# Second halves of two-engine operations are put off to the next background step, in a two-part transformer kernel on one core

## The chip, the cores and the metric

The kernel runs on one core of one Trainium2 chip, in one launch. The metric is device microseconds from start to end of the launch, lower is better. TensorE is called PE in the profile, VectorE DVE, ScalarE ACT, GpSimd POOL and SyncE SP.

## The reference

One sequence of 512 tokens of width 1024 goes through two stacks, all in fp32. The first has two layers, each with a feed-forward block, a hybrid mixer (causal attention with forget gates beside a depthwise convolution), a second feed-forward block and a gated per-layer embedding. The second has four branches, one each: a state-space layer (s5), sliding-window attention (swa), causal attention with latent queries and keys (mla) and a spatial gating unit (sgu). Cut to its frame:

```python
def first_block(x, p, ...):
    h = x
    for i in range(2):
        h = h + 0.5 * swiglu(rmsnorm(h, g_ff1[i]), w_ff1_in[i], w_ff1_out[i])
        h = h + hybrid_mixer(rmsnorm(h, g_mix[i]), w_in[i], ...)
        h = h + 0.5 * swiglu(rmsnorm(h, g_ff2[i]), w_ff2_in[i], w_ff2_out[i])
        h = h + sigmoid(rmsnorm(h, g_ple[i]) @ w_ple_gate[i]) * (p[i] @ w_ple_proj[i])
    return rmsnorm(h, g_final)

def second_block(x, ...):
    for i, branch in enumerate((s5, swa, mla, sgu)):
        x = x + rmsnorm(branch(rmsnorm(x, pre_norm[i])), post_norm[i])
    return x
```

swiglu has 2816 hidden channels, so its second product sums over 22 blocks of 128.

## The kernel before, in words

Activations lie transposed, as 8 tiles of 128 channels by 512 tokens (`h`), and every dense product is made of 128x128 weight blocks against 512 tokens. To keep fp32 accuracy each operand is split into a high part and a low part, and each block product is three matmuls (`mm3`): L449 high weight by high data, L450 high weight by low data, L451 low weight by high data.

**Weights** are streamed in units of 8 blocks. `_dma` loads a unit into `raw` (three buffers). `_split` makes the two parts: ACT copies it into `whi` (L406), then DVE subtracts to get `wlo` (L407 in the code; in the profile all DVE operations go through one wrapper and show as L248). The two parts have three buffers each. `block` hands out the next block; when a unit is used up, `_advance` goes to the next unit and first calls `_ahead`, which splits up to two units beyond the one that starts.

**Epilogues** follow the tiles: after the matmuls of one output tile, `after_tile` runs small chains of DVE and ACT operations on its result. Many of them end in `split` (ACT makes the high part, DVE the low part), so that the next product can use the result. In the second product of a feed-forward block the epilogue adds the tile to `h` on DVE and then prepares the next block's operand (`prep`): high part on ACT (L715), low part on DVE, square on ACT, sum on DVE.

**Background steps.** Generators (attention, convolution, the scan of s5) are advanced by `step` after each tile and by `fine`, which `mtile` calls after the blocks 1, 3 and 5 of a tile, but only of a tile of 6 or 8 blocks. The 22-block tiles of the second feed-forward product call neither inside a tile. Neither does the head of `tiles`: there, after the branches s5, swa and mla, the first three tiles of the next branch are computed for the first 256 tokens, one after the other, and between them `one`, `two` and `rest` issue the norm of the branch before for the other 256 tokens; then the three tiles are computed for those (L514 to L527).

**Order.** The program is scheduled by hand: each engine executes its instructions in the order in which the Python code issues them. An instruction whose operand isn't ready holds up all that stand behind it on its engine. So the place at which the code issues an instruction is the place it has in its queue.

Of the kernel before, what the change touches and what calls it, by code (L numbers as in the profile page):

```python
# [291 lines left out]
class Kern:  # L292
# [3 lines left out]
    def __init__(self, ctx, tc, t, outT):  # L296
        self.tc, self.nc, self.t, self.outT = tc, tc.nc, t, outT
        nc = self.nc
        self.v = Vector(self, nc.vector)
        self.pe_n = self.dve_n = 0.0  # L300
        self.force = False
        pool = lambda n, b, **k: ctx.enter_context(tc.tile_pool(name=n, bufs=b, **k))
        self.cp = pool("const", 1)
        self.rawp = pool("raw", 3)
        self.wp = pool("wsplit", 3)
        self.sp = pool("slots", 1)
        self.smp = pool("small", 4)
# [18 lines left out]
        self.tables, self.M8, self.tabbed = {}, {}, []  # L326


# [64 lines left out]
    def _split(self):  # L393
        i = self.spli
        r = self.raws.pop(i)
        if self.units[i][1]:
            hl = self.slots(2), self.slots(2)
            self.kept.append(hl)
        else:
            hl = [[self.wp.tile([P, UB * P], F32, tag=n, name=self.nm(n))] for n in ("whi", "wlo")]  # L400
        self.sps[i] = self.r(hl)
        self.spli += 1
        w = UB * P // len(hl[0])

        def piece(hi, lo, src):
            self.nc.scalar.copy(hi.bitcast(F32R), src)  # L406
            self.v.tensor_tensor(lo.bitcast(F32R), src, hi, op=ALU.subtract)  # L407
        if i == 0:
            a, b = slice(0, w // 2), slice(w // 2, w)
            piece(hl[0][0][:, a], hl[1][0][:, a], r[:, a])  # L410
            return lambda: piece(hl[0][0][:, b], hl[1][0][:, b], r[:, b])
        for j, (hi, lo) in enumerate(zip(*hl)):
            piece(hi, lo, r[:, j * w:(j + 1) * w])
# [12 lines left out]
    def _advance(self, hold=0):  # L426
        self._ahead(self.ui, hold)
        self.cur = self.sps.pop(self.ui)
        self.ui += 1
        self.blkpos = 0  # L430
# [118 lines left out]
    def step(self):  # L549
# [5 lines left out]
        self.fine()  # L555

    def fine(self):
        for g in list(self.fines):
            if next(g, self) is self:
                self.fines.remove(g)  # L560
# [17 lines left out]
    def run_hooks(self):  # L578
        while self.hooks:
            self.hooks.popleft()()  # L580
        self.flush()
        while self.lazy:
            self.lazy.popleft()()


    def split(self, src, hi, lo, scale=None):
# [4 lines left out]
        else:  # L591
            nc.scalar.activation(hi.bitcast(F32R), src, AF.Copy, scale=scale)  # L592
            self.v.scalar_tensor_tensor(out=lo.bitcast(F32R), in0=src, scalar=scale, in1=hi,
                                           op0=ALU.mult, op1=ALU.subtract)

    @staticmethod
    def r(hl):
# [3 lines left out]

    def silu(self, ps, times=1.0):
# [3 lines left out]
        self.v.scalar_tensor_tensor(out=y, in0=t, scalar=1.0, in1=y, op0=ALU.add, op1=ALU.mult)  # L606
        self.free(t)
        return y

# [237 lines left out]
    def mixer(self, l, nxt):  # L847
# [61 lines left out]
        for p in range(4):  # L909
            for dst, sc in ((Q, -0.125), (K, None)):  # L910
                ps = self.mtile(Xr)

                def epi(ps=ps, dst=dst, sc=sc):
                    t, hi, lo = self.slot(), self.slot(), self.slot()
                    v.tensor_tensor(t, ps, self.rbc, op=ALU.mult)
                    self.split(t, hi, lo, sc)
                    self.free(t)
                    dst.append((hi, lo))
                self.after_tile(epi)
# [69 lines left out]
    def causal(self, n, ready, can_pv, begin, score, values, lags):  # L989
        nc, v = self.nc, self.v  # L990
        C = (self.slot(), self.slot())
        for t in C:
            nc.gpsimd.memset(t[:, 0:P], 0.0)
        todo, box, own = {}, {}, {}

# [3 lines left out]
        def scores(h, i):  # L999
# [5 lines left out]
            pr = own[h][0][:, P:] if i == 2 else own[h][-1]  # L1005
            mn, sm = (self.small([P, 1], tag=n, bufs=8) for n in ("mn", "sm"))
            score(h, i, pr, mn)
            box[h][0].append(pr)
            box[h][1].append((mn, sm))

        def exp(h, i):
            pr, (mn, sm) = box[h][0][i], box[h][1][i]
# [39 lines left out]
        while h < n or todo:  # L1052
            if h < n and t >= start and ready(h):
                at(t, begin, h)
                for i in range(4):
                    at(t + 1 + i, scores, h, i)
                    at(t + 2 + i, exp, h, i)
                    at(t + 3 + i, divide, h, i)
                for j in range(3):
# [14 lines left out]
    def attn(self, Q, K, V, decay, O):  # L1074
# [36 lines left out]
        def values(h, po):  # L1111
# [4 lines left out]
            def epi():  # L1116
                if h % 2 == 0:
                    half.append((self.slot(), self.slot()))
                self.split(po[rows], half[p][0][rows], half[p][1][rows])
                if h % 2:  # L1120
                    O.append(half[p])
            return epi, [(self.r(x)[0][:, c], self.r(x)[1][:, c]) for x in V]
# [376 lines left out]
    def s5(self, nxt):  # L1499
# [54 lines left out]
        def finish(m):  # L1554
# [5 lines left out]
            nc.scalar.activation(U[m], U[m], AF.Gelu_apprx_tanh)  # L1560
            self.split(U[m], hi, lo)
            Y.append((hi, lo))
            self.free(yr)
# [31 lines left out]
        for ps in tl:  # L1595

            def epi(ps=ps):
                Z.append(self.silu(ps, 0.5))
            self.after_tile(epi)
# [4 lines left out]
        for m, ps in enumerate(self.led(Y, KD, KD)):  # L1604
            def epi(ps=ps, m=m):
                s, hi, lo = self.slot(), self.slot(), self.slot()
                nc.scalar.activation(s, ps, AF.Tanh, scale=0.5, bias=half[:, m:m + 1])
                v.scalar_tensor_tensor(out=s, in0=s, scalar=1.0, in1=Z[m], op0=ALU.add, op1=ALU.mult)
                v.tensor_tensor(s, s, U[m], op=ALU.mult)
                self.split(s, hi, lo)  # L1610
                self.free(s, Z[m], U[m])
                M.append((hi, lo))
            self.after_tile(epi)
# [5 lines left out]
    def swa(self, nxt):  # L1619
# [16 lines left out]
        def project(ps, scale, dst):  # L1636
            def epi():
                t, hi, lo = self.slot(), self.slot(), self.slot()
                v.tensor_tensor(t, ps, self.rbc, op=ALU.mult)
                self.split(t, hi, lo, scale)  # L1640
                self.free(t)
                dst.append((hi, lo))
            self.after_tile(epi)
# [20 lines left out]
        def gate_in(ps):  # L1664
            def epi():
                Z.append(self.silu(ps))
            self.after_tile(epi)
# [99 lines left out]
        def gate(p, e):  # L1767
# [5 lines left out]
            if e:  # L1773
                hi, lo = self.slot(), self.slot()
                self.split(Z[p], hi, lo)
                self.free(Z[p])
                M.append((hi, lo))

# [38 lines left out]
    def mla(self, nxt):  # L1817
# [17 lines left out]
        def latent(n, gname, st, out, done=None):  # L1835
            for m in range(n):
                def epi(ps=next(tl), m=m):
                    t, hi, lo = self.slot(), self.slot(), self.slot()
                    v.tensor_tensor(t, ps, self.rbc, op=ALU.mult)
                    self.split(t, hi, lo, self.vec(gname, m))  # L1840
                    self.stat_add(st, t)
                    self.free(t)
                    out.append((hi, lo))
                    if done is not None and m == n - 1:
# [52 lines left out]
        def values(h, po):  # L1897
# [5 lines left out]
            def epi():  # L1903
                v.tensor_tensor(Z[p][rows], Z[p][rows], po[rows], op=ALU.mult)
                if h % 2:
                    M.append((self.slot(), self.slot()))
                    self.split(Z[p], *M[p])
                    self.free(Z[p])
                if h % 4 == 3:
# [6 lines left out]
        for p in range(8):  # L1916
            if p % 2 == 0:
# [9 lines left out]
                def split_v(vps=vps, hl=hl):  # L1927
                    for i in range(4):
                        yield
                        c = slice(i % 2 * 256, (i % 2 + 1) * 256)  # L1930
                        self.split(vps[i // 2][:, c], hl[0][i // 2][:, c], hl[1][i // 2][:, c],
                                   box["kvc"][:, i:i + 1])
                self.fines.append(split_v())
                V[p // 2] = hl
            for h in (2 * p, 2 * p + 1):
                ps = self.mtile(Qr)

                def epi(ps=ps, h=h):
                    t, hi, lo = self.slot(), self.slot(), self.slot()
                    v.tensor_tensor(t, ps, (tE, tO)[h % 2], op=ALU.mult)  # L1940
                    self.split(t, hi, lo)
                    self.free(t)
                    QH[h] = (hi, lo)
# [3 lines left out]
            def epi(ps=ps, p=p):  # L1947
                t = self.slot()
                v.tensor_tensor(t, ps, box["kvb"], op=ALU.mult)
                tt = (self.slot(), self.slot())  # L1950
                self.split(t, *tt)
                while len(scored) < 2 * p - 2:
                    self.fine()
                for h in (2 * p, 2 * p + 1):
                    for a, b in zip(KS[h % 4], tt):
                        nc.sync.dma_start(a[nope(h)], b[nope(h)])
                    ready[h] = self.tick
                self.free(t, tt)
            self.after_tile(epi)
        self.free(*CQ, *CKV, tEO)  # L1960
        self.post_out(M, 2, nxt)
# [191 lines left out]
```

## Time and profile before

| | |
|---|---|
| median of 3 runs | 3349.96 us (3349.73 to 3351.64) |
| profiled execution, own time | 3348.41 us |
| its span, first to last instruction | 3346.6 us |
| PE busy | 3273.1 us, 98% of the span |
| DVE busy | 2089.7 us, 62% |
| ACT busy | 1286.2 us, 38% |
| POOL busy | 431.9 us, 13% |
| mean granted clock of TensorE | 0.991 |

The profile is that of one execution. A busy share is an average over the whole span; an instruction's row in the timeline has its start, its duration, and in brackets the idle time of its engine before it and what ended it. A matmul's duration overlaps with the next one's: the spacing of starts is what counts.

### The profile page before, as it was taken

The numbers are of one execution on the slowest core, as the hardware profiler recorded it, in microseconds if no ns is written. First come the engines' busy times: TensorE is split into PE (matmuls) and PEld (weight loads), VectorE is DVE, ScalarE is ACT, GpSimd is POOL, SyncE is SP. The second block draws the span as 40 slices with busy tenths as digits, with TensorE's granted clock in tenths as the row PEclk, the third lists the DMA queues.
The fourth block names the chain that finished last, engine by engine and source line by source line (L and its number), as shares of the span: only waits on it lengthen the run. The fifth ranks groups of instructions, "written<-read, shape, count | busy, mean of one in ns | idle before, by whom it ended". The sixth has DMA issues, their size and how long they took to land. (4 is left out here: it accounts for less than half of the span.)

```text
span 3346.6 us, 42633 instructions
## 1 busy us (share of the span) xinstructions
PE 3273.1 (98%) x16016; PEld 2723.6 (81%) x16016; DVE 2089.7 (62%) x4056; ACT 1286.2 (38%) x2186; POOL 431.9 (13%) x558
## 2 busy tenths in 40 slices
PE   9999999999999999999999999998999999999997
PEld 7888777888888888887778888887888788788887
DVE  6653488766653676536887654346666666676665
ACT  4322334433332433323434422224443554455433
POOL 0100013001100011000220000001102332043201
PEclk9999999999999999999999999999999999999998
DMA  5433221224432244322222333335632112322221
GB/s 179 134 112 101 89 95 63 94 88 140 138 117 97 92 132 137 118 97 91 86 66 92 112 112 101 113 126 160 202 108 85 64 64 75 109 73 69 83 82 64
DMA packets 120302, 348.09 MB, mean 104 GB/s; under 512 B 30560, under 2 KB 33280, under 8 KB 120096
## 3 DMA queue, kind: packets, MB, share of 16 engines
q1 hardware_dynamic: 103824, 295.68, 27.2%
q0 software_dynamic: 16272, 49.69, 4.4%
q8 instruction: 126, 2.06, 0.3%
q14 instruction: 80, 0.66, 0.1%
HBM read 312.75 MB, written 28.11 MB: 102 GB/s over the span
## 5 line engine op out<-in xcount | busy, mean ns | idle before, releaser
L449 PE MATMUL mm<-s,whi 128*128 128x512 f32 (+1 forms) x3528 | 1383.7, 392 | 14.0 <-ACT s L715 7.1
L451 PE MATMUL mm<-s,wlo 128*128 128x512 f32 (+1 forms) x3528 | 1364.4, 387 | 6.0 <-DVE wlo L248 6.0
L450 PE MATMUL mm<-s,whi 128*128 128x512 f32 (+1 forms) x3528 | 1365.3, 387 | 3.6 <-DVE s L248 3.2
L248 DVE TENSOR_TENSOR wlo<-raw,whi 128x1024 fp32r<-128x1024 f32 (+1 forms) x488 | 594.5, 1224 | 522.2 <-ACT whi L406 518.1
L449 PEld LDWEIGHTS mm<-s,whi 128*128 128x128 f32 x3528 | 665.9, 189 | 150.4 <-ACT s L715 7.4
L451 PEld LDWEIGHTS mm<-s,wlo 128*128 128x128 f32 x3528 | 665.1, 189 | 144.3 <-DVE wlo L248 10.0
L450 PEld LDWEIGHTS mm<-s,whi 128*128 128x128 f32 x3528 | 666.0, 189 | 134.4 <-DVE s L248 8.2
L406 ACT CAST whi<-raw 128x1024 fp32r<-128x1024 f32 (+1 forms) x488 | 507.6, 1044 | 554.5 <-PE mm L450 273.0
L248 DVE TENSOR_TENSOR s<-s,s 128x512 f32<-128x512 f32 (+7 forms) x888 | 436.9, 518 | 156.7 <-ACT s L589 129.1
L248 DVE TENSOR_TENSOR s<-mm,rbc 128x512 f32<-128x512 f32 x296 | 199.8, 687 | 189.8 <-PE mm L451 168.9
L589 ACT CAST s<-s 128x512 fp32r<-128x512 f32 x189 | 115.1, 616 | 378.5 <-DVE s L248 378.3
L1021 POOL TENSOR_SCALAR s<-s,m 128x128 f32<-128x128 f32 (+3 forms) x128 | 152.2, 1193 | 502.7 <-DVE m L248 312.1
L248 DVE SCALAR_TENSOR_TENSOR s<-s,vecs,s 128x511 f32<-128x511 f32 (+13 forms) x256 | 180.7, 748 | 10.3 <-ACT s L592 6.7
L449 PE MATMUL sd<-s,s 128*128 128x256 f32 (+2 forms) x472 | 158.6, 336 | 8.3 <-ACT s L592 3.6
L822 ACT ACTIVATE s<-s 128x512 f32<-128x512 f32 x88 | 55.7, 633 | 251.7 <-DVE s L248 251.7
L450 PE MATMUL sd<-s,s 128*128 128x256 f32 (+2 forms) x472 | 146.4, 310 | 2.3 <-DVE s L248 1.5
L451 PE MATMUL sd<-s,s 128*128 128x256 f32 (+2 forms) x472 | 145.0, 307 | 0.0
L449 PE MATMUL mm<-s,s 128*128 128x256 f32 x448 | 130.8, 292 | 11.4 <-ACT s L589 10.9
L715 ACT ACTIVATE s<-h,vecs 128x512 fp32r<-128x512 f32 (+1 forms) x112 | 70.9, 633 | 182.6 <-DVE h L248 182.6
L449 PEld LDWEIGHTS sd<-s,s 128*128 128x128 f32 (+1 forms) x472 | 90.1, 191 | 54.8 <-issue 20.4
L450 PE MATMUL mm<-s,s 128*128 128x256 f32 x448 | 128.8, 288 | 2.3 <-DVE s L248 2.0
L451 PE MATMUL mm<-s,s 128*128 128x256 f32 x448 | 127.9, 285 | 0.3 <-DVE s L248 0.3
(210 smaller groups left out, 3344.2 us busy)
## 6 DMA issues: line engine op xcount, KB each, us to landing
raw<-in_mix_dram SPq DMA_DIRECT2D x104, 512.0 KB, 3.3
raw<-in_ff2i_dram SPq DMA_DIRECT2D x88, 512.0 KB, 3.3
raw<-in_ff1i_dram SPq DMA_DIRECT2D x87, 512.0 KB, 3.4
raw<-in_ff1o_dram SPq DMA_DIRECT2D x44, 512.0 KB, 3.3
raw<-in_ff2o_dram SPq DMA_DIRECT2D x44, 512.0 KB, 3.3
raw<-in_mlaw_dram SPq DMA_DIRECT2D x33, 512.0 KB, 3.3
tab<-s POOLq DMA_DIRECT2D x64, 256.0 KB, 2.3
s<-tab POOLq DMA_DIRECT2D x64, 256.0 KB, 5.6
```

The source lines that it names most:

```text
L248: return f(*a, **kw)
L406: self.nc.scalar.copy(hi.bitcast(F32R), src)
L449: mm(ps, wh, xh, start=first, stop=False)
L450: mm(ps, wh, xl, start=False, stop=False)
L451: mm(ps, wl, xh, start=False, stop=last)
L589: nc.scalar.copy(hi.bitcast(F32R), src)
L715: self.nc.scalar.activation(hi.bitcast(F32R), src, AF.Copy, scale=gv)
L822: nc.scalar.activation(sg, ta, AF.Silu)
L1021: nc.gpsimd.tensor_scalar(out=pr[:, c], in0=pr[:, c], scalar1=ri, scalar2=None, op0=ALU.mult)
```

## The change

A queue `soons` is added. `soon(f)` puts a piece of work there; `fine` now first issues what stands in the queue; `settle` issues all of it at once. Where an operation has a first half on one engine and a second half on another, the second half now goes to this queue. This holds for the low part of a weight unit unless the unit is needed next (`_advance` calls `settle` if the unit that starts is still without its low part); for the low part in the epilogues of the mixers and of the s5, swa and mla branches (`split_soon`); and for the last step of `silu`. The epilogue of the second feed-forward product keeps its order. In `causal`, the row sums of two query blocks now stand side by side, so that one reciprocal serves both; the two divisions on POOL follow it together. Operands get lists or names of their own only when they are complete. The core of the diff:

```diff
         def piece(hi, lo, src):
             self.nc.scalar.copy(hi.bitcast(F32R), src)
-            self.v.tensor_tensor(lo.bitcast(F32R), src, hi, op=ALU.subtract)
+            def rest():
+                self.v.tensor_tensor(lo.bitcast(F32R), src, hi, op=ALU.subtract)
+                self.unsplit.discard(i)
+            if i > max(self.ui, 1):
+                self.unsplit.add(i)
+                self.soon(rest)
+            else:
+                rest()
...
     def _advance(self, hold=0):
         self._ahead(self.ui, hold)
+        if self.ui in self.unsplit:
+            self.settle()
         self.cur = self.sps.pop(self.ui)
...
+    def soon(self, f):
+        self.soons.append(f)
+
+    def settle(self):
+        while self.soons:
+            self.soons.popleft()()
+
     def fine(self):
+        for _ in range(len(self.soons)):
+            if self.soons:
+                self.soons.popleft()()
         for g in list(self.fines):
...
+    def split_soon(self, src, hi, lo, scale=None, then=None):
+        if scale is None:
+            self.nc.scalar.copy(hi.bitcast(F32R), src)
+        else:
+            self.nc.scalar.activation(hi.bitcast(F32R), src, AF.Copy, scale=scale)
+
+        def rest():
+            if scale is None:
+                self.v.tensor_tensor(lo.bitcast(F32R), src, hi, op=ALU.subtract)
...
+            if then is not None:
+                then()
+        self.soon(rest)
...
         def divide(h, i):
-            pr, (_, sm) = box[h][0][i], box[h][1][i]
-            c = slice(0, (i + 1) * P)
-            ri = self.small([P, 1], tag="ri", bufs=8)
-            v.reciprocal(ri, sm)
-            nc.gpsimd.tensor_scalar(out=pr[:, c], in0=pr[:, c], scalar1=ri, scalar2=None, op0=ALU.mult)
+            s2, r2 = box[h][1][i][3]
+            v.reciprocal(r2, s2)
+            for i in (i - 1, i):
+                pr, ri = box[h][0][i], box[h][1][i][2]
+                c = slice(0, (i + 1) * P)
+                nc.gpsimd.tensor_scalar(out=pr[:, c], in0=pr[:, c], scalar1=ri, scalar2=None, op0=ALU.mult)
```

How it moves instructions shows at two places. The numbers behind names tell buffers apart and differ between the two programs.

First place: DVE in the second product of the first feed-forward block, around the end of its fourth tile (`mm_2415`; `mm_2502` is the fifth). `h_83` is the fourth tile's sum, `s_2496` its low part, `s_2413` the sum of squares. Before:

```order
L248 SCALAR_TENSOR_TENSOR h_82<-mm_2323,h_82 128x512
L248 SCALAR_TENSOR_TENSOR s_2410<-h_82,vecs,s_2409 128x512
L248 TENSOR_TENSOR wlo_2435<-raw_2340,whi_2434 128x1024
L248 TENSOR_TENSOR wlo_2465<-raw_2370,whi_2464 128x1024
L248 SCALAR_TENSOR_TENSOR h_83<-mm_2415,h_83 128x512
L248 SCALAR_TENSOR_TENSOR s_2496<-h_83,vecs,s_2495 128x512
L248 TENSOR_TENSOR s_2413<-s_2413,s_2499 128x512
L248 TENSOR_TENSOR wlo_2504<-raw_2400,whi_2503 128x1024
```

The same stretch in the changed program:

```order
L248 SCALAR_TENSOR_TENSOR h_82<-mm_2323,h_82 128x512
L248 SCALAR_TENSOR_TENSOR s_2410<-h_82,vecs,s_2409 128x512
L248 SCALAR_TENSOR_TENSOR h_83<-mm_2415,h_83 128x512
L248 SCALAR_TENSOR_TENSOR s_2494<-h_83,vecs,s_2493 128x512
L248 TENSOR_TENSOR s_2413<-s_2413,s_2497 128x512
L248 TENSOR_TENSOR wlo_2435<-raw_2339,whi_2434 128x1024
L248 TENSOR_TENSOR wlo_2464<-raw_2368,whi_2463 128x1024
L248 TENSOR_TENSOR wlo_2504<-raw_2397,whi_2503 128x1024
```

The low parts of two weight units have moved behind the epilogue of the fourth tile. The first of them, `wlo_2435`, is the unit with which the fifth tile begins; PE's order is the same in both programs, and the third matmul of that tile reads it:

```order
L451 MATMUL mm_2415<-s_2135,wlo_2397 128x512
L449 MATMUL mm_2502<-s_323,whi_2434 128x512
L450 MATMUL mm_2502<-s_324,whi_2434 128x512
L451 MATMUL mm_2502<-s_323,wlo_2435 128x512
L449 MATMUL mm_2502<-s_380,whi_2434 128x512
```

These are PE's rows there: the last of the fourth tile and the first of the fifth. Nothing moved on this engine.

Second place: DVE in the head of `tiles` between s5 and swa, where `wlo_19885` is the unit of the third head tile. Before, it stood ahead of the 38 DVE operations of `one`, `two` and `rest`, of which the first (`m_19919`) is here:

```order
L248 TENSOR_TENSOR h_87<-h_87,s_19223 128x256
L248 SCALAR_TENSOR_TENSOR s_19810<-h_86,vecs,s_19809 128x256
L248 SCALAR_TENSOR_TENSOR s_19846<-h_87,vecs,s_19845 128x256
L248 TENSOR_TENSOR wlo_19885<-raw_19427,whi_19884 128x1024
L248 TENSOR_SCALAR m_19919<-sd_19914 128x2
L248 TENSOR_SCALAR m_19922<-m_19919 128x2
```

In the changed program the same unit is called `wlo_19789`, and stands behind the last of those 38 (the low part of `h_87` for the second 256 tokens):

```order
L248 SCALAR_TENSOR_TENSOR s_19705<-h_85,vecs,s_19704 128x256
L248 TENSOR_TENSOR h_87<-h_87,s_19126 128x256
L248 SCALAR_TENSOR_TENSOR s_19714<-h_86,vecs,s_19713 128x256
L248 SCALAR_TENSOR_TENSOR s_19750<-h_87,vecs,s_19749 128x256
L248 TENSOR_TENSOR wlo_19789<-raw_19329,whi_19788 128x1024
L248 TENSOR_SCALAR m_20032<-vecs 128x16
```

PE's order is again the same up to the end of swa: the third head tile for the first 256 tokens, whose third matmul reads this low part, comes before all matmuls for the other 256 tokens.

## Rows read from the trace of the kernel before

**Rows 1.** The page, busy time by engine.

```profile
PE 3273.1 (98%) x16016; PEld 2723.6 (81%) x16016; DVE 2089.7 (62%) x4056; ACT 1286.2 (38%) x2186; POOL 431.9 (13%) x558
```

**Rows 2.** Waits of PE: line, what it waited for, us, times, longest.

```profile
PE mm L451 <- DVE wlo L248: 6.0, 7, 1.4
PE mm L450 <- DVE s L248: 5.2, 18, 0.4
...
PE sd L451 <- DVE wlo L248: 2.8, 6, 0.5
```

**Rows 3.** Timeline of DVE around the end of the fourth 22-block tile.

```profile
307.81 1.23 DVE L248 TENSOR_TENSOR wlo<-raw,whi 128x1024 fp32r<-128x1024 f32 x1 [2.07 <-ACT whi L406]
...
317.79 0.69 DVE L248 SCALAR_TENSOR_TENSOR h<-mm,h 128x512 f32<-128x512 f32 x1 [3.31 <-PE mm L451]
319.28 0.75 DVE L248 SCALAR_TENSOR_TENSOR s<-h,vecs,s 128x512 fp32r<-128x512 f32 x1 [0.79 <-ACT s L715]
319.95 0.69 DVE L248 TENSOR_TENSOR s<-s,s 128x512 f32<-128x512 f32 x1
```

**Rows 4.** Timeline of PE at the start of the fifth tile.

```profile
317.82 0.39 PE L450 MATMUL mm<-s,whi 128*128 128x512 f32 x1
318.05 0.39 PE L451 MATMUL mm<-s,wlo 128*128 128x512 f32 x1
```

**Rows 5.** Timeline of DVE at the end of the eighth tile.

```profile
377.63 0.69 DVE L248 SCALAR_TENSOR_TENSOR h<-mm,h 128x512 f32<-128x512 f32 x1 [3.31 <-PE mm L451]
379.12 0.75 DVE L248 SCALAR_TENSOR_TENSOR s<-h,vecs,s 128x512 fp32r<-128x512 f32 x1 [0.79 <-ACT s L715]
```

**Rows 6.** Timeline of PE at the first unit of the mixer.

```profile
377.88 0.39 PE L451 MATMUL mm<-s,wlo 128*128 128x512 f32 x1
```

**Rows 7.** Timeline of DVE in the head between s5 and swa, first and last.

```profile
2546.25 1.23 DVE L248 TENSOR_TENSOR wlo<-raw,whi 128x1024 fp32r<-128x1024 f32 x1 [0.69 <-ACT whi L406]
...
2562.24 0.70 DVE L248 SCALAR_TENSOR_TENSOR s<-h,vecs,s 128x256 fp32r<-128x256 f32 x1 [0.18 <-ACT s L715]
```

**Rows 8.** Timeline of PE, third head tile, first 256 tokens.

```profile
2551.38 0.28 PE L451 MATMUL mm<-s,wlo 128*128 128x256 f32 x1
```

**Rows 9.** Timeline of PE: first instructions behind idle times.

```profile
407.19 0.50 PE L451 MATMUL mm<-s,wlo 128*128 128x512 f32 x1 [1.40 <-DVE wlo L248]
...
2327.62 3.65 PE L1518 MATMUL sd<-s,s 128*128 128x64 f32 x16 [3.24 <-DMA s<-ud]
...
2733.91 0.58 PE L449 MATMUL mm<-s,s 128*128 128x256 f32 x1 [2.03 <-ACT s L589]
...
3050.57 0.50 PE L449 MATMUL sd<-s,s 128*128 128x512 f32 x1 [1.97 <-DVE s L248]
```

**Rows 10.** Stretches: us; busy of PE, PEld, DVE, ACT, POOL; clock; DMA; GB/s.

```profile
407.20:414.00 6.80, 6.80 (x30) 5.65 (x31) 6.45 (x9) 4.10 (x6) 0.00 (x0) 1.00 0.65 205
2327.60:2334.40 6.80, 6.78 (x24) 6.13 (x25) 1.86 (x3) 1.16 (x2) 0.54 (x1) 0.50 0.62 139
2587.10:2597.30 10.20, 10.20 (x27) 7.71 (x28) 7.16 (x14) 4.04 (x7) 0.00 (x0) 0.50 0.16 51
2734.00:2740.60 6.60, 6.31 (x25) 5.44 (x26) 2.64 (x8) 2.36 (x8) 1.37 (x2) 0.50 0.01 2
3051.30:3054.60 3.30, 3.30 (x14) 2.98 (x14) 2.99 (x12) 1.31 (x4) 2.27 (x3) 0.50 0.44 159
```

**Rows 11.** Timeline of PE inside the stretch that began at 2327.62.

```profile
2333.73 0.63 PE L449 MATMUL mm<-s,whi 128*128 128x512 f32 x1
2334.16 0.53 PE L450 MATMUL mm<-s,whi 128*128 128x512 f32 x1
```

**Rows 12.** Timelines of DVE and of PE in the first gated embedding.

```profile
1135.41 0.69 DVE L248 TENSOR_TENSOR s<-s,s 128x512 f32<-128x512 f32 x1
...
1134.98 0.39 PE L451 MATMUL mm<-s,wlo 128*128 128x512 f32 x1
```

**Rows 13.** Stretch of mla's attention, columns as in rows 10.

```profile
2905.00:3067.00 162.00, 156.34 (x901) 137.50 (x900) 117.81 (x319) 91.20 (x222) 62.70 (x59) 0.99 0.26 76
```

More of the change, by code (lines that the diff above doesn't have):

```diff
@@ L326, in __init__ @@
         self.tables, self.M8, self.tabbed = {}, {}, []
+        self.soons, self.unsplit = deque(), set()
     def pe(self, n, passes=1):
@@ L583, in run_hooks @@
             self.lazy.popleft()()
+        self.settle()
     def split(self, src, hi, lo, scale=None):
@@ L594, in split @@
                                            op0=ALU.mult, op1=ALU.subtract)
+    def split_soon(self, src, hi, lo, scale=None, then=None):
[6 more added lines that the diff above has]
+                self.v.tensor_tensor(lo.bitcast(F32R), src, hi, op=ALU.subtract)
+            else:
+                self.v.scalar_tensor_tensor(out=lo.bitcast(F32R), in0=src, scalar=scale, in1=hi,
+                                            op0=ALU.mult, op1=ALU.subtract)
+            if then is not None:
+                then()
+        self.soon(rest)
+    HALVES = slice(0, 64), slice(64, P)
     @staticmethod
@@ L599, in r, with silu @@
         return f(hl[0]), f(hl[1])
-    def silu(self, ps, times=1.0):
+    def silu(self, ps, times, then):
         y, t = self.slot(), self.slot()
@@ L605, in silu, with rest @@
         self.nc.scalar.activation(t, y, AF.Tanh, scale=1.0 / times)
-        self.v.scalar_tensor_tensor(out=y, in0=t, scalar=1.0, in1=y, op0=ALU.add, op1=ALU.mult)
-        self.free(t)
-        return y
+        def rest():
+            self.v.scalar_tensor_tensor(out=y, in0=t, scalar=1.0, in1=y, op0=ALU.add, op1=ALU.mult)
+            self.free(t)
+            then(y)
+        self.soon(rest)
     def stat_add(self, st, src, scale=None, c=slice(0, T), pool=False, apart=False):
@@ L915, in epi @@
                     v.tensor_tensor(t, ps, self.rbc, op=ALU.mult)
-                    self.split(t, hi, lo, sc)
-                    self.free(t)
-                    dst.append((hi, lo))
+                    self.split_soon(t, hi, lo, sc, lambda: (self.free(t), dst.append((hi, lo))))
                 self.after_tile(epi)
@@ L993, in causal @@
             nc.gpsimd.memset(t[:, 0:P], 0.0)
-        todo, box, own = {}, {}, {}
+        todo, box, own, two = {}, {}, {}, {}
         def at(k, f, *a):
@@ L1005, in scores @@
             pr = own[h][0][:, P:] if i == 2 else own[h][-1]
-            mn, sm = (self.small([P, 1], tag=n, bufs=8) for n in ("mn", "sm"))
+            mn = self.small([P, 1], tag="mn", bufs=8)
+            if i % 2 == 0:
+                two[h] = [self.small([P, 2], tag=n, bufs=6) for n in ("sm", "ri")]
+            sm, ri = (x[:, i % 2:i % 2 + 1] for x in two[h])
             score(h, i, pr, mn)
             box[h][0].append(pr)
-            box[h][1].append((mn, sm))
+            box[h][1].append((mn, sm, ri, two[h]))
         def exp(h, i):
-            pr, (mn, sm) = box[h][0][i], box[h][1][i]
+            pr, (mn, sm, *_) = box[h][0][i], box[h][1][i]
             c = slice(0, (i + 1) * P)
@@ L1057, in causal @@
                     at(t + 2 + i, exp, h, i)
-                    at(t + 3 + i, divide, h, i)
+                    if i % 2:
+                        at(t + 3 + i, divide, h, i)
                 for j in range(3):
@@ L1118, in epi @@
                     half.append((self.slot(), self.slot()))
-                self.split(po[rows], half[p][0][rows], half[p][1][rows])
-                if h % 2:
-                    O.append(half[p])
+                self.split_soon(po[rows], half[p][0][rows], half[p][1][rows], None,
+                                lambda: h % 2 and O.append(half[p]))
             return epi, [(self.r(x)[0][:, c], self.r(x)[1][:, c]) for x in V]
@@ L1560, in finish @@
             nc.scalar.activation(U[m], U[m], AF.Gelu_apprx_tanh)
-            self.split(U[m], hi, lo)
-            Y.append((hi, lo))
+            self.split_soon(U[m], hi, lo, None, lambda: Y.append((hi, lo)))
             self.free(yr)
@@ L1597, in epi @@
             def epi(ps=ps):
-                Z.append(self.silu(ps, 0.5))
+                self.silu(ps, 0.5, Z.append)
             self.after_tile(epi)
@@ L1607, in epi, with rest @@
                 nc.scalar.activation(s, ps, AF.Tanh, scale=0.5, bias=half[:, m:m + 1])
[L1608 to L1612, printed above, removed]
+                def rest():
+                    v.scalar_tensor_tensor(out=s, in0=s, scalar=1.0, in1=Z[m], op0=ALU.add, op1=ALU.mult)
+                    v.tensor_tensor(s, s, U[m], op=ALU.mult)
+                    self.split_soon(s, hi, lo, None, lambda: (self.free(s, Z[m], U[m]), M.append((hi, lo))))
+                self.soon(rest)
             self.after_tile(epi)
@@ L1639, in epi @@
                 v.tensor_tensor(t, ps, self.rbc, op=ALU.mult)
-                self.split(t, hi, lo, scale)
-                self.free(t)
-                dst.append((hi, lo))
+                self.split_soon(t, hi, lo, scale, lambda: (self.free(t), dst.append((hi, lo))))
             self.after_tile(epi)
@@ L1665, in epi @@
             def epi():
-                Z.append(self.silu(ps))
+                self.silu(ps, 1.0, Z.append)
             self.after_tile(epi)
@@ L1774, in gate @@
                 hi, lo = self.slot(), self.slot()
-                self.split(Z[p], hi, lo)
-                self.free(Z[p])
-                M.append((hi, lo))
+                self.split_soon(Z[p], hi, lo, None, lambda: (self.free(Z[p]), M.append((hi, lo))))
         def attend():
@@ L1839, in epi @@
                     v.tensor_tensor(t, ps, self.rbc, op=ALU.mult)
-                    self.split(t, hi, lo, self.vec(gname, m))
+                    self.split_soon(t, hi, lo, self.vec(gname, m), lambda: (self.free(t), out.append((hi, lo))))
                     self.stat_add(st, t)
-                    self.free(t)
-                    out.append((hi, lo))
                     if done is not None and m == n - 1:
@@ L1905, in epi @@
                 if h % 2:
-                    M.append((self.slot(), self.slot()))
-                    self.split(Z[p], *M[p])
-                    self.free(Z[p])
+                    x = self.slot(), self.slot()
+                    self.split_soon(Z[p], *x, None, lambda: (self.free(Z[p]), M.append(x)))
                 if h % 4 == 3:
@@ L1930, in split_v @@
                         c = slice(i % 2 * 256, (i % 2 + 1) * 256)
-                        self.split(vps[i // 2][:, c], hl[0][i // 2][:, c], hl[1][i // 2][:, c],
-                                   box["kvc"][:, i:i + 1])
+                        self.split_soon(vps[i // 2][:, c], hl[0][i // 2][:, c], hl[1][i // 2][:, c],
+                                        box["kvc"][:, i:i + 1])
                 self.fines.append(split_v())
@@ L1940, in epi @@
                     v.tensor_tensor(t, ps, (tE, tO)[h % 2], op=ALU.mult)
-                    self.split(t, hi, lo)
-                    self.free(t)
+                    self.split_soon(t, hi, lo, None, lambda: self.free(t))
                     QH[h] = (hi, lo)
@@ L1950, in epi, with rest @@
                 tt = (self.slot(), self.slot())
[L1951 to L1958, printed above, removed]
+                def rest():
+                    while len(scored) < 2 * p - 2:
+                        self.fine()
+                    for h in (2 * p, 2 * p + 1):
+                        for a, b in zip(KS[h % 4], tt):
+                            nc.sync.dma_start(a[nope(h)], b[nope(h)])
+                        ready[h] = self.tick
+                    self.free(t, tt)
+                self.split_soon(t, *tt, None, rest)
             self.after_tile(epi)
+        self.settle()
         self.free(*CQ, *CKV, tEO)
```

## The prediction, as put on record before the changed kernel ran

> **What bounds the kernel now.** I read the page first: PE is busy 98% of the span [rows 1], so time can be gained only where PE stands idle, and any new idle time of PE is lost time. Next the waits of PE by what ended them: the waits for DVE on which the change bears are small, 6.0 and 2.8 us for the low part of weights (L451) and 5.2 us for low parts of data (L450), 14.0 us in all [rows 2]. Then I took the two programs' orders and looked up, in the timeline of before, each instruction that now stands behind others. Engines go in order, so an instruction that is put behind one that waits for PE can't start before that wait is over. In the rows the reader is to see how near the later place comes to the matmul that reads the result.
>
> **Step A, the end of the fourth of eight tiles in each second feed-forward product (4 places).** A tile has 22 blocks and a unit 8, so two units that are split inside the fourth tile have no background step until that tile's epilogue has been issued. Before, the first of them was done at 307.81 + 1.23 = 309.04 [rows 3], 9.0 us before PE read it at 318.05 [rows 4]. Now it stands behind three operations of the epilogue, and these wait for the tile's last matmul: they run at 317.79, 319.28 and 319.95, the last until 320.64 [rows 3]. The low part takes 1.23 us and ends at 321.87. PE reaches its matmul at 318.05 whatever DVE does, and waits 321.87 - 318.05 = 3.82 us. The unit behind it, 1.23 us later, is read only 24 matmuls later, 24 x 0.23 = 5.5 us [rows 4], and costs nothing. The ACT copy of the unit isn't moved; DVE is what is late. Four feed-forward blocks: 4 x 3.82 = **15.3 us**.
>
> **Step B, the end of the eighth tile (4 places).** The same chain stands at 377.63 and 379.12 [rows 5], 59.84 us after step A's, and PE reads the first unit of the next phase at 377.88 [rows 6], 59.83 us after its matmul of step A. So again 3.82 us, and 4 x 3.82 = **15.3 us**.
>
> **Step C, the head of `tiles` after s5, swa and mla (3 places).** The third unit's low part ran at 2546.25 [rows 7], 3.9 us before its use at 2551.38 [rows 8]. Now it stands behind the 38 operations of `one`, `two` and `rest`, since the head calls no background step and only the advance to that unit settles it. The last of the 38 ends at 2562.24 + 0.70 = 2562.94 [rows 7]; they don't come earlier, as they wait for PE's norm sums and for each other. With 1.23 us the low part ends at 2564.17: 12.79 us of idle PE. Something is given back: when PE goes on, the other 256 tokens' operands are all ready, while before PE met short waits of 5.2/18 = 0.29 us there [rows 2], three per head, 0.9 us. So 11.9 us each, 3 x 11.9 = **35.7 us**.
>
> **The clock behind each wait.** Idle times of 3.24, 2.03 and 1.97 us [rows 9] were each followed by a granted clock of 0.50, which is 1.2 of 2.4 GHz, for 6.80, 6.60 and 3.30 us, and the idle time before 2587.10 by 10.20 us of it; behind 1.40 us the clock stayed at 1.00 [rows 9, 10]. The 11 waits of A to C are all longer than those that lowered it. At the half clock matmuls of 512 columns start 0.43 us apart [rows 11], else 0.23 [rows 4]: 0.47 of a stretch is lost. The four stretches have a mean of 6.7 us, hence 3.2 us for one and 11 x 3.2 = **35.2 us**; the ends are 0 (no fall) and 10.2 x 0.47 = 4.8 us each, 53 us.
> The Trainium skill (TensorE: Matmul & The Clock Gate, section HAM oscillation — how this bites in real kernels) speaks against waits of this kind: a wait between bursts makes the next burst start cold, and it counts half of the throttled time as lost, by which the term would be 11 x 3.4 = 37 us, an estimate. The rows give 0.47 rather than half; the sum goes by the rows.
>
> **Step D, the gated embeddings (2 places).** Here deferred units stand behind the epilogue of a tile. By the old times one would end at 1135.41 + 0.69 + 1.23 = 1137.33, and PE reads it at 1134.98 [rows 12]: at most 2.35 us. But the epilogue itself starts up to 1.2 us earlier, because the low part no longer stands ahead of it. In the second layer two more additions of 0.69 stand there, so up to 3.7 us. Bounds 0 and 6.1 us; I take 3, the middle, as the chain is partly bound by PE's tile and partly by DVE itself.
>
> **The rest.** In the mixers, s5 and swa the moved low parts of queries change places with convolution or scan operations of about 0.7 us which used to run behind them, and these fill DVE's wait for ACT; the end stays within a few tenths. I take 0, bounds -2 and +2. In mla the order of attention against projections changes on PE too; its attention stretch has 162.00 - 156.34 = 5.7 us of idle PE [rows 13], which bounds the gain. For the loss, later queries may double these waits, and a fall of clock or two may join: +12. I take 0. The 64 reciprocals that go were on DVE beside busy PE: 0. The divisions that POOL now does in pairs start later by one block; the same stretch's bounds hold them.
>
> **Sum.** 15.3 + 15.3 + 35.7 + 35.2 + 3 = 104.5 us on the profiled execution's 3348.41, that is 3452.9. The median of the runs is 1.55 us above that execution, so 3454.5, say **3455 us**, 3.1% slower.
>
> **Rivals.**
> 1. The waits come, the clock doesn't fall. For it: 1.40 us of idle left the clock alone. Against: every longer one inside the program that I looked at lowered it [rows 9, 10]. 3455 - 35 = 3420 us.
> 2. The waits and longer half-clock stretches, with mla and step D at their bad ends: 17.6 + 12 + 3 more, 3487 us.
> 3. Faster. DVE is no longer held up by ACT's first halves, so what PE waits for from DVE comes early: the 14.0 us of rows 2 go, 3336 us. The mechanism has its place in the mixers, swa and mla. It decides only if steps A to C cost less than it gives, that is if the low part in step A ended before 318.05. Against it: in-order DVE can't pass an epilogue that waits until 317.79 for PE.
> 4. The change does not do what it says where it matters (the deferred parts come in time after all, at the next background step): within a few us of 3350. Against it: neither the 22-block tiles nor the head have a background step inside.
>
> **How the numbers follow.** The forecast, 0.68; rival 1, 0.15; rival 2, 0.10; rival 3, 0.04; rival 4, 0.03. The range goes from rival 1 with step D at 0, 3417, to rival 2, 3487, and leaves out rivals 3 and 4 and some of the edges. A measurement of this kernel can tell 0.2%, 6.7 us, from no change. Slower by more than that: 0.68 + 0.15 + 0.10 = 0.93 and the worse part of rival 4, 0.94 in all; faster 0.03; same 0.03.
>
> **What would show it.** Right, if the changed profile has four waits of PE for `wlo` of about 3.8 us at the fifth tiles and four at the ends of the second feed-forward products, three of about 12.8 us in the heads, PE's busy time grown by some 35 us through stretches at clock 0.50 right behind them, and a mean clock near 0.98. In the waits by releaser, L451 for `wlo` should go from 8.8 to about 77 us and more. Step A is wrong if `wlo` at the fifth tile runs before the epilogue; the clock term is wrong if the stretches behind the waits show 1.00. The prediction as a whole is wrong if the time stays below 3400 us: then the waits aren't there, or the attention stages gave back more than rows 2 and 13 hold.

## The result, and the profile after

The changed kernel takes **3438.24 us** (median of 4 runs, 3432.53 to 3439.85) against 3350.39 before (3349.73 to 3351.64): ratio 1.0257, interval 1.0244 to 1.027. The forecast was 3455, range 3417 to 3487. The profiled execution took 3437.43 us, its span is 3435.7, the mean granted clock 0.978 instead of 0.991.

The page's line of busy times, to be held against [rows 1]:

```profile
PE 3291.7 (96%) x16016; PEld 2738.8 (80%) x16016; DVE 2079.6 (61%) x3992; ACT 1284.9 (37%) x2186; POOL 432.5 (13%) x558
```

The span grew by 89.1 us. PE's busy time grew by 18.6 although it has the same 16016 matmuls: that is time at the half clock (a granted clock of 0.50). The other 70.5 us are idle PE. The waits of PE, as in [rows 2] (its lines L449 to L451 are now L459 to L461), say for what:

```profile
PE mm L461 <- DVE wlo L248: 68.9, 17, 13.0
PE sd L461 <- DVE wlo L248: 10.0, 8, 3.6
...
PE mm L460 <- DVE s L248: 2.8, 7, 0.8
```

The wait for the low part of weights went from 8.8 to 78.9 us; forecast were about 77 and more. The timeline of DVE at the end of the fourth 22-block tile, the place of [rows 3]:

```profile
319.08 0.69 DVE L248 SCALAR_TENSOR_TENSOR h<-mm,h 128x512 f32<-128x512 f32 x1 [12.05 <-PE mm L461]
320.56 0.75 DVE L248 SCALAR_TENSOR_TENSOR s<-h,vecs,s 128x512 fp32r<-128x512 f32 x1 [0.79 <-ACT s L759]
321.23 0.68 DVE L248 TENSOR_TENSOR s<-s,s 128x512 f32<-128x512 f32 x1
321.83 3.49 DVE L248 TENSOR_TENSOR wlo<-raw,whi 128x1024 fp32r<-128x1024 f32 x3
```

DVE stands idle for 12.05 us ahead of the epilogue. Before, two low parts of weights were made in that time; now three are made in a row behind it. PE, at the same place and in the head between s5 and swa:

```profile
319.11 0.39 PE L460 MATMUL mm<-s,whi 128*128 128x512 f32 x1
323.11 0.50 PE L461 MATMUL mm<-s,wlo 128*128 128x512 f32 x1 [3.61 <-DVE wlo L248]
...
2597.26 0.28 PE L460 MATMUL mm<-s,whi 128*128 128x256 f32 x1
2610.58 0.58 PE L461 MATMUL mm<-s,wlo 128*128 128x256 f32 x1 [13.04 <-DVE wlo L248]
```

The first wait counted in starts is 323.11 - 319.11 - 0.23 = 3.77 us, the second 2610.58 - 2597.26 - 0.12 = 13.20 us (0.23 and 0.12 are the usual spacing of starts at 512 and 256 columns; the bracket counts from the end of the matmul before). All eight waits of steps A and B have 3.61 in the bracket to within 0.01 and all three of step C 13.03 or 13.04.

Now the clock behind the waits: stretches of the changed kernel, columns as in [rows 10], behind the first wait of step A, the second of step A, the second of step B, and the first two of step C.

```profile
323.20:326.60 3.40, 3.40 (x11) 2.77 (x12) 2.12 (x2) 0.00 (x0) 0.00 (x0) 0.71 0.64 199
326.70:330.00 3.30, 3.30 (x13) 2.70 (x12) 0.00 (x0) 0.15 (x1) 0.00 (x0) 0.80 0.68 263
1050.20:1053.50 3.30, 3.30 (x15) 2.73 (x16) 2.13 (x2) 0.00 (x0) 0.00 (x0) 1.00 0.54 182
1053.60:1057.00 3.40, 3.40 (x16) 2.81 (x16) 0.67 (x1) 1.05 (x1) 0.00 (x0) 1.00 0.76 283
1113.90:1117.30 3.40, 3.40 (x8) 2.72 (x9) 3.29 (x4) 0.00 (x0) 1.05 (x2) 0.50 0.66 200
1117.30:1120.70 3.40, 3.40 (x11) 2.62 (x11) 0.17 (x1) 0.00 (x0) 0.00 (x0) 0.61 0.70 233
2610.70:2614.00 3.30, 3.30 (x16) 3.30 (x17) 0.44 (x1) 0.00 (x0) 1.13 (x2) 0.50 0.45 159
2861.20:2864.60 3.40, 3.40 (x18) 3.40 (x18) 0.00 (x0) 0.00 (x0) 2.16 (x4) 0.57 0.46 154
```

A stretch of length L with mean clock c holds L(1 - c)/0.5 at the half clock. Behind the first wait that is 2.0 + 1.3 = 3.3 us; behind the second none at all; behind the third 3.4 + 2.7 = 6.1; over all 11 waits 0 to 6.1, with a mean of 3.3 us.

This is one execution. The eight waits of A and B come again, 3.61 us long and ahead of the same instructions, in two runs below: that with only the heads mended and that with the weights' deferral alone. The half clock falls differently there. The second wait of step A has none here and some in the first of these runs; the third of step A has 1.9 + 1.5 us here and none in the second. The third wait of step A here, the second of step A with only the heads mended, and the third of step A with the weights' deferral alone:

```profile
1487.10:1490.50 3.40, 3.40 (x11) 2.77 (x12) 2.16 (x2) 0.00 (x0) 0.00 (x0) 0.72 0.71 192
```

```profile
1053.30:1056.70 3.40, 3.40 (x10) 2.69 (x11) 2.18 (x2) 0.00 (x0) 0.00 (x0) 0.66 0.60 183
```

```profile
1486.20:1489.60 3.40, 3.40 (x15) 2.81 (x16) 2.21 (x2) 0.00 (x0) 0.00 (x0) 1.00 0.72 186
```

So neither a wait's length nor its place settles what the clock does behind it. The sums differ less: 26, 31 and 26 us of half clock behind the eight waits in the three profiles.

Where the 89 us are, found by comparing the start of the same PE instruction in both traces:

| place | forecast, us | measured, us |
|---|---|---|
| A and B, idle and clock | 30.6 + 25.6 | 28.9 + 14.8 |
| C, idle (net) and clock | 35.7 + 9.6 | 36.5 + 1.8 |
| D, gated embeddings | 3 | -0.8 |
| mla's attention stage | 0 | 3.5 idle + 4.8 clock |
| all else | 0 | -0.8 |
| sum | 104.5 | 88.7 |

(Idle is the sum of the brackets, less in C the short waits that went. The clock is what the starts say beyond that: it holds also the 0.16 us by which starts say more for each wait and, in C, what PE gained besides behind the waits. "All else" hides two larger terms that cancel: s5 is 3.8 us longer in this profile and swa, up to the head behind it, 4.3 us shorter.)

### The profile page after: what moved, and what is told of

Same layout as the page of the kernel before. It is cut to its first block, busy times and chain, and to the rows that moved or that the text cites. A ratio compares the mean times of both kernels' runs of the same rounds, so it can differ in the third digit from the quotient of the medians.

```text
span 3435.7 us, 42488 instructions
## 1 busy us (share of the span) xinstructions
PE 3291.7 (96%) x16016; PEld 2738.8 (80%) x16016; DVE 2079.6 (61%) x3992; ACT 1284.9 (37%) x2186; POOL 432.5 (13%) x558
## 5 line engine op out<-in xcount | busy, mean ns | idle before, releaser
L461 PE MATMUL mm<-s,wlo 128*128 128x512 f32 (+1 forms) x3528 | 1369.5, 388 | 68.9 <-DVE wlo L248 68.9
L459 PE MATMUL mm<-s,whi 128*128 128x512 f32 (+1 forms) x3528 | 1387.5, 393 | 21.3 <-DVE s L248 8.8
L461 PEld LDWEIGHTS mm<-s,wlo 128*128 128x128 f32 x3528 | 669.1, 190 | 211.3 <-DVE wlo L248 75.8
L459 PEld LDWEIGHTS mm<-s,whi 128*128 128x128 f32 x3528 | 669.5, 190 | 157.7 <-DVE s L248 9.6
L611 ACT CAST s<-s 128x512 fp32r<-128x512 f32 (+1 forms) x125 | 75.5, 614 | 265.2 <-DVE s L248 265.2
L459 PE MATMUL sd<-s,s 128*128 128x256 f32 (+2 forms) x472 | 160.7, 341 | 6.0 <-ACT s L623 3.6
L461 PE MATMUL sd<-s,s 128*128 128x256 f32 (+2 forms) x472 | 146.2, 310 | 0.3 <-DVE s L248 0.3
L459 PE MATMUL mm<-s,s 128*128 128x256 f32 x448 | 130.8, 292 | 9.0 <-ACT s L621 4.9
L248 DVE TENSOR_TENSOR s<-sd,s 128x512 fp32r<-128x512 f32 (+5 forms) x186 | 94.7, 535 | 63.4 <-ACT s L1075 41.1
L459 PEld LDWEIGHTS sd<-s,s 128*128 128x128 f32 (+1 forms) x472 | 92.0, 195 | 50.8 <-issue 22.1
L460 PE MATMUL mm<-s,s 128*128 128x256 f32 x448 | 129.0, 288 | 2.0 <-DVE s L248 1.7
```

The source lines that it names most:

```text
L248: return f(*a, **kw)
L459: mm(ps, wh, xh, start=first, stop=False)
L460: mm(ps, wh, xl, start=False, stop=False)
L461: mm(ps, wl, xh, start=False, stop=last)
```

## The experiments

Each run's time is compared with the kernel before on the same chip; there the kernel before took 3351.3 to 3352.1 us, against 3350.4 beside the changed kernel, so a difference from the changed kernel carries up to 2 us of that, beside the spread of the runs. A place is called mended where the deferred work is issued early enough again that PE doesn't wait for it.

**The weights' low parts issued at once, all else as changed.**

```diff
-            if i > max(self.ui, 1):
+            if False:
```

> The changed kernel with one thing undone: the low part of every weight unit is issued at once, as before; the other deferrals and the paired division stay. Theory (the waits of steps A to C carry the loss): by the trace of the changed kernel steps A and B add 43.7 us (28.9 idle, 14.8 half clock) and step C 38.2 us; both go, and 3438 - 82 = 3356 us is left, 6 us above before, from mla, where the changed trace is 8.3 us longer. PE's waits for wlo fall from 79 to about 9 us. Rival (the deferred epilogue halves cost as much): above 3380 us. Other rival (they gain, and the weights alone hide it): below 3347 us.

Measured: 3357.8 us, ratio 1.0019 (1.0009 to 1.0028). The waits for wlo are back at 10.0 us:

```profile
PE mm L461 <- DVE wlo L248: 7.2, 7, 2.3
...
PE sd L461 <- DVE wlo L248: 2.8, 6, 0.5
```

So 80 of the 88 us come from deferring the weights' low parts. The 6.4 us that this run is slower than the kernel before are beyond its interval, and about as many as expected. Its profile is of the slowest of its ten runs (3364.0 us); there mla's attention stage is 8.6 us longer than before, 5.0 of it idle PE, and s5 6.0 us longer. So the deferred epilogue halves don't gain; what they cost is taken up below.

**Only the heads mended.**

```diff
+                self.settle()
                 if j == 0:
                     one()
```

> The changed kernel with all deferred work issued in the head of each branch before the norm of the branch before (step C alone mended). Theory: the three waits of 13.0 us go and nothing takes their place, 3438 - 38 = 3400 us; PE's waits for wlo in mm tiles fall from 69 to about 30 us. Rival: the other 256 tokens' operands come later by the low part's 1.23 us and PE waits there instead, or the half-clock time moves elsewhere; above 3410 us.

Measured: 3399.0 us, ratio 1.014 (1.0125 to 1.0155), 39 less than the changed kernel. The waits of PE:

```profile
PE mm L461 <- DVE wlo L248: 30.1, 15, 3.6
PE sd L461 <- DVE wlo L248: 10.0, 8, 3.6
...
PE mm L460 <- DVE s L248: 4.9, 17, 0.3
```

Nothing took the place of the three long waits but the short ones that were there before the change: the last line is back near its 5.2 us of [rows 2].

**Only the 22-block tiles mended.**

```diff
                 (self.step if k == 3 else self.fine)()
+            elif n == KF and k % 8 == 7:
+                self.settle()
```

> The changed kernel with deferred work issued after blocks 7 and 15 inside the 22-block tiles (steps A and B alone mended). Theory: eight waits of 3.6 us go with the half clock behind them, 3438 - 44 = 3394 us, and the clock is 1.00 at the starts of the fifth tiles. Rival (the half clock there has another cause): only the idle 29 us go, 3409 us.

Measured: 3394.6 us, ratio 1.0128 (1.0113 to 1.0143), 44 less. Against the changed kernel's trace, the eight places lose 3.61 us of idle each and together 14.9 us more, as the theory had it.

**The waits of A and B shortened, not removed.**

```diff
                                                op0=ALU.mult, op1=ALU.add)
+                self.settle()
                 self.prep(m)
```

> The changed kernel with the deferred weight parts issued right after the tile's sum, ahead of its low part and square (steps A and B shortened). Theory: the eight waits shrink from 3.6 to about 1.45 us, which is 17 us, and since the trace of before shows 1.40 us of idle without a fall of the clock, the 14.8 us of half clock go too: 3406 us. Rival (any pause lowers the clock there): 3421 us.

Measured: 3408.2 us, ratio 1.0171 (1.0154 to 1.0188), 30 less than the changed kernel. The first shortened wait, and stretches behind the first of step A and the second of step B, where the long wait had left 0.71 and 0.50:

```profile
320.02 0.50 PE L461 MATMUL mm<-s,wlo 128*128 128x512 f32 x1 [1.47 <-DVE wlo L248]
```

```profile
320.00:323.40 3.40, 3.38 (x15) 2.77 (x16) 3.40 (x4) 1.04 (x2) 0.00 (x0) 1.00 0.55 194
...
323.40:326.80 3.40, 3.40 (x17) 2.81 (x16) 0.66 (x2) 1.05 (x1) 0.00 (x0) 1.00 0.80 257
...
1101.10:1104.50 3.40, 3.38 (x15) 2.79 (x16) 3.19 (x5) 2.09 (x4) 0.18 (x1) 1.00 0.68 195
```

The wait shrank by 2.14 us, and the saving was 3.6 to 3.8 us at six places, 5.0 at the second of step B, where the half clock had lasted longest, and 2.1 at the second of step A, where there had been none. So the half clock belongs to the long wait. A wait of 1.47 us did not bring it in any of the eight.

**All three steps mended; and then the epilogues of mla too.** Head and tile edits together:

> The changed kernel with steps A, B and C mended together (deferred work issued in the heads and after blocks 7 and 15 of the 22-block tiles); low parts of weights stay deferred everywhere else. Theory (the three steps are independent and hold nearly all of the loss): 3438 - 82 = 3356 us; a few us less than with all weights issued at once (3358), since in the trace of the changed kernel the norm chains behind the feed-forward blocks, the embeddings and the mixers gained 3 us: 3354. Rival (the weights' deferral gains nothing anywhere): 3358 or more.

Measured: 3349.4 us, ratio 0.9997 (0.9988 to 1.0006). The loss is gone, and no gain is left. On top of this, the values' low parts at once:

```diff
-                        self.split_soon(vps[i // 2][:, c], hl[0][i // 2][:, c], hl[1][i // 2][:, c],
+                        self.split(vps[i // 2][:, c], hl[0][i // 2][:, c], hl[1][i // 2][:, c],
```

> As the run with A to C mended, and in mla the low part of the value tiles is issued at once again. Theory: the deferred low parts read the value tiles in PSUM, hold the mm buffers longer and make PE wait at the start of the next projection tiles (waits of 1.5, 1.2, 2.8 and 2.8 us for DVE in the changed kernel, at 2966 to 3083 us); with them and the half clock behind them gone, 6 us less than with A to C mended alone, about 3348. Rival (mla loses by the later queries and keys, or by the paired division): no change, 3354.

Measured: 3351.4 us, ratio 1.0 (0.9992 to 1.0009): no 6 us. Then every deferred half in mla at once (five `split_soon` calls back to `split`):

> As the run with A to C mended, and in mla every deferred epilogue half (latents, values, queries, keys with their DMAs, outputs) is issued at once again; the paired division stays. Theory (mla's loss is by the deferred epilogues): the 8 us of the changed trace's mla stage go, 3346. Rival (it is by the paired division, after which PE waits for POOL and for the row's reciprocal): 3352 or more.

Measured: 3350.1 us, ratio 0.9997 (0.9988 to 1.0006). The theory that 8 us were to be had with A to C mended falls. PE's idle time in mla's attention stage, from the same instruction to the same instruction, is 10.8 us before, 14.3 in the changed kernel, 14.7 with A to C mended and 11.9 with mla undone as well. So the deferred epilogues do cost that stage some 3 us of idle, too little for these times. The other 5 us of the changed kernel's mla stage were clock: with A to C mended they were 0.7 us, in the run with the weights issued at once 3.6. Why that run loses 6 us and the one with A to C mended none stays open.

**The paired division alone, on the kernel before.**

> The kernel before with the paired reciprocal and division alone. Theory: the divisions start a block later; where PE has projections to do that is hidden, and at the end of mla, where it has none, it costs about 1.25 us; the swa branch has its row sums in no pair code, so nothing changes there. 3350 to 3353. Rival (the pairing is what cost mla 8 us): 3357 or more. Other rival (fewer DVE instructions gain): 3347 or less.

Measured: 3352.0 us, ratio 0.9998 (0.9989 to 1.0007). In its profile mla's stage is 0.5 us longer. But its span is 4.8 us longer than that of the kernel before, and the other 4.3 lie in s5, which this edit doesn't touch: s5 has 6.8 us more at the half clock there, and 1.5 us more idle. Single profiles differ by some 4 us in s5 without a cause in the code, and that of the kernel before has the shortest s5 of all twelve.

**The weights' deferral alone, on the kernel before.**

> The kernel before with one thing added: the low parts of weight units are deferred to the next background step, as in the change; every epilogue and the division stay as before. Theory (the weights' low parts carry the loss by themselves): before + 82 us for A to C, less some 3 us at norm chains and embeddings, 3429 us, with 11 waits of 3.6 and 13 us for wlo. Rival (the waits need the deferred epilogue halves as well): below 3400 us.

Measured: 3437.1 us, ratio 1.0258 (1.0243 to 1.0274), the changed kernel's ratio. Its waits for wlo:

```profile
PE mm L461 <- DVE wlo L248: 68.0, 17, 13.0
...
PE sd L461 <- DVE wlo L248: 10.0, 8, 3.6
```

The weights' deferral is enough for the whole loss, and without it 80 us of the loss go. The time is 8 us above the expected 3429; in this profile s5 is 5.3 us longer than before, and the half clock behind the second and third waits of step C lasts 5.9 us each instead of 2.9.

**The same, with A to C mended.**

> The kernel before with the low parts of weight units deferred, and issued in the heads and after blocks 7 and 15 of the 22-block tiles, so that A to C don't arise. Theory: what the deferral of weights gives where it doesn't stall PE, 0.5 us at two norm chains, 0.4 us at each embedding and 0.9 us at the end of the second: about 3 us below before, less than can be told apart. Rival (it gains in swa and mla too): 3344 us or less.

Measured: 3354.6 us, ratio 1.0009 (1.0 to 1.0018). The 3 us of gain are not there. Its profile does have 0.5 us less at each of two norm chains in either layer, 0.4 at each embedding and 0.9 behind the second, but s5 is longer by 5.8 us and mla by 3.7. No version was found that beats the kernel before.

## Why the prediction was right

**Steps A and B** held: forecast 3.82 us for each wait, measured 3.77 in starts at the first and 3.61 in the brackets of all eight. Mending the 22-block tiles alone took all of them away.

**Step C** held: forecast 12.79 us, measured 13.20 in starts. The 0.4 us more are the low part itself, which took 1.74 us there (the rows are in the last section) and not the 1.23 of [rows 7]. With 0.9 us given back the forecast had 35.7 us for three; the idle time grew by 36.5.

**The clock** is the term that was mis-sized. The step "the four stretches have a mean of 6.7 us, hence 3.2 us for one and 11 x 3.2 = 35.2 us" took its length from [rows 10]. Behind the 11 new waits the half clock lasted 3.3 us on average; 11 x 3.3 x 0.47 = 17 us, and by the starts it cost 14.8 + 1.8 = 16.6 us, about half of the term. PE's busy time, forecast to grow by some 35 us, grew by 18.6, with mla's share in it. The direction was right: the shortened waits show that it's the long wait that brings the half clock. But one of the eight waits of 3.61 us brought none, and another one in another run, so the sentence that every longer wait lowers the clock was too strong. The same goes for a wait of 2.27 us in the first feed-forward product of the changed kernel, longer than two in [rows 9] that lowered it:

```profile
93.37 0.50 PE L461 MATMUL mm<-s,wlo 128*128 128x512 f32 x1 [2.27 <-DVE wlo L248]
```

```profile
93.40:96.80 3.40, 3.40 (x15) 2.83 (x16) 2.94 (x4) 0.95 (x2) 0.00 (x0) 1.00 0.68 210
```

What in the stretches of before made them twice as long wasn't tried. The prediction's first step, that time can be gained only where PE stands idle, left the clock out too: a stretch at 0.50 counts as busy PE and loses 0.47 of its length.

The sentence cited from the Trainium skill (TensorE: Matmul & The Clock Gate, section HAM oscillation — how this bites in real kernels), that half of the throttled time is lost, agrees with the trace roughly: 11 x 3.3 = 36 us at the half clock would cost 18 us by it, an estimate, and by the starts they cost 16.6. That the next burst starts cold, also cited there, the trace bears out for 5 of the 11 waits, the three of step C and two of step B; behind five the clock was still 1.00 when PE went on, and behind one it stayed there.

**Step D** was bounded from 0 to 6.1 us and taken at 3; it came out at -0.8. Waits for `wlo` did come, two of 0.94 and 0.93 us in the second layer and one of 0.18 in the first, but more was given back: in the second layer the wait of 1.68 us for `whi` went. The changed kernel, then the kernel before:

```profile
2312.50 0.50 PE L461 MATMUL mm<-s,wlo 128*128 128x512 f32 x1 [0.94 <-DVE wlo L248]
2319.16 0.50 PE L461 MATMUL mm<-s,wlo 128*128 128x512 f32 x1 [0.93 <-DVE wlo L248]
```

```profile
2297.56 0.50 PE L449 MATMUL mm<-s,whi 128*128 128x512 f32 x1 [1.68 <-ACT whi L406]
```

**The rest**: mla had bounds -5.7 and +12 and came out at +8.3 in this profile, of which 3.5 us are idle time. With A to C mended the runs put about 3 us of idle on the deferred epilogue halves and 0.5 us on the paired division; their effect on the time is below what these runs can tell. The stages of s5 and swa were taken at 0. This profile has 3.8 us more in s5, with 2.3 us more idle and 6.8 us more at the half clock, and 4.3 us less in swa, with 7.4 us less at the half clock; that they cancel is luck.

**The sum.** From the forecast 104.5 us to the 88.7 found, the clock behind A to C is 18.6 us short, step D 3.8, the idle times of A to C 0.9 and all else 0.8; mla's 8.3 us, taken at 0, run against them. Without that second error the sum would have been 24 us off instead of 16: the step from the waits to their idle time was right, and the nearness of the total is in part luck.

**Rivals.** Rival 3 fell: with A to C mended, where its gain would have shown, the time is that of before. Rival 1 fell by the half clock behind ten of the 11 waits. Rival 2 asked for longer half-clock stretches than the forecast had, and they were shorter. Rival 4 fell by the 11 waits.

## What to carry to other kernels

On an in-order engine, putting work off to "the next background step" is safe only where such a step comes before the next instruction that waits: look for the stretches without one (long inner loops, hand-written heads), and for each deferred instruction compare the end of what now stands ahead of it with the start of its first reader. Work that an engine did while it waited for another was free; moved behind that wait, it stands on the path at full length. A wait's price is its length plus what the clock loses after it, and that second part is known only to a factor of two from other stretches; at one and the same wait it was 0 in one run and 3.4 us at the half clock in another.

## What of the hardware was not expected

In the heads the low part of a weight unit took 1.74 us instead of 1.23, and POOL's additions beside it took longer too. DVE and POOL in the changed kernel's head between s5 and swa:

```profile
2608.78 1.74 DVE L248 TENSOR_TENSOR wlo<-raw,whi 128x1024 fp32r<-128x1024 f32 x1
```

```profile
2607.37 0.81 POOL L670 TENSOR_TENSOR s<-s,s 128x256 f32<-128x256 f32 x1 [0.40 <-ACT s L666]
2608.58 3.33 POOL L670 TENSOR_TENSOR s<-s,s 128x256 f32<-128x256 f32 x3 [0.40 <-ACT s L666]
```

The three additions took 1.11 us each on average, an earlier one 0.81. The same 1.74 stands in the other two heads. The traces speak for it that the two engines slow each other: of the weight units' low parts of this size that have no POOL operation beside them, over 400 in either kernel's trace, none took more than 1.23 us. In the kernel before, two in a row took 3.45 us (1.23 and 2.31) beside POOL's additions of 128x512, about as long as the three in a row at 321.83 of the changed kernel's first timeline, which had no POOL operation beside them. The kernel before, DVE and POOL in the last branch:

```profile
3182.99 3.45 DVE L248 TENSOR_TENSOR wlo<-raw,whi 128x1024 fp32r<-128x1024 f32 x2 [3.19 <-ACT whi L406]
```

```profile
3180.53 7.05 POOL L2060 TENSOR_TENSOR s<-s,s 128x512 f32<-128x512 f32 x4 [36.05 <-ACT s L2058]
```

No run was made to test it.

Behind the first wait of 3.61 us the clock didn't fall at once: it was 1.00 for the first microsecond of matmuls, and 0.50 from two microseconds after the wait. Behind the second wait of step B it was 0.50 from the first matmul on:

```profile
323.10:324.10 1.00, 0.99 (x4) 0.86 (x5) 1.00 (x1) 0.00 (x0) 0.00 (x0) 1.00 0.12 12
...
325.10:326.10 1.00, 1.00 (x4) 0.81 (x3) 0.22 (x1) 0.00 (x0) 0.00 (x0) 0.50 0.80 287
```

```profile
1113.80:1115.00 1.20, 1.15 (x3) 0.96 (x4) 1.20 (x2) 0.00 (x0) 0.00 (x0) 0.50 0.34 41
```
